# Opening stage of a hybrid decoder step: operands made kind by kind between the products of two blocks, second token half turned through a scaled identity

## The chip, the cores and the metric

One core of one Trainium2 chip. The metric is the device time of one execution in microseconds (us). The kernel before takes 2243.91 us, the median of 3 runs (2242.6 to 2245.94).

## What is computed

One inference step of a decoder trunk with one layer, for 1024 prompt tokens and 32 sample tokens (8 sequences of 4), all float32. In the reference, cut to what the opening touches:

```
h = rmsnorm(x, norm_w)                                       # x: tokens x 1024
pool_in, pool_z, qk_pre, v, o_pre, m_z, if_pre, gate_pre = jnp.split(h @ w_in, SPLIT_OFFSETS, axis=-1)
...
qk, conv_hist_new = causal_conv_silu(qk_pre, conv_hist, conv_w, conv_b)   # 4 taps along the tokens, then silu
q, k = jnp.split(qk, 2, axis=-1)
```

with `rmsnorm(x, w) = x * rsqrt(mean(x * x) + EPS) * w`, the mean over the 1024 features of a token. Behind it stand a pooling branch, a matrix memory (mLSTM) over chunks of 128 tokens, gates, an output projection and a last norm. `w_in` is 1024 features by some 12,000 columns, and the kernel goes through it in blocks of 256 columns.

## The kernel before, in words

**Tokens and halves.** The tokens are cut into two halves of 512 prompt and 16 sample tokens, HH = 528 columns each (`early` and `late`). The 1024 features are 8 tiles of 128 partitions (k = 0 to 7), and h stands with the features on the partitions.

**Products.** A block of w_in (1024 features by 256 columns) is multiplied with all tokens by a scheme of seven products in place of eight: both matrices are cut into 2 x 2 parts, and sums and differences of the parts are multiplied. `OPS` names the h operand of each: product a takes B11 (early tokens, features 0 to 511), 00 takes B21 (early, features 512 to 1023), d takes M1 = B12 - B11 (B12 and B22 are the late tokens' parts), b takes M2 = M1 - B22, c takes T3 = B22 - B12, 10 takes N4 = M2 + B21, 01 takes B22. The weights are combined in `prep`.

**Precision.** Each operand is split into a high part in fp32r and the rest: weights into whi and wlo, h into hh and hl (M2 into m2h and m2l, T3 into t3h and t3l, N4 into n4h and n4l). The high part is made on ScalarE (ACT, `hi`, L363 and L365), the low one on VectorE (DVE, `lo`, L369 and L371). High by high, high by low and low by high are multiplied. With 4 tiles of features and 2 token pieces of 264 (CH) a product is 24 TensorE (PE) matmuls in a FeatBlock (L157: the blocks of q and k, whose output has the columns on the partitions) and 48 in a block of the other form (L215, 256 columns). The first two blocks, 0 and 1, are FeatBlocks of q, ConvBlocks: their results go through the conv (`give`: L315 on ACT, three taps L317 on DVE, the silu L320 and L321 on ACT, then a store).

**The opening.** `norm_in` (L522) loads the four early x tiles of 128 tokens, scales each row by its rstd (L550), turns them on PE (L554, transposes, 4 per k) and splits them into hh and hl; it also keeps a copy of each turned tile, r1 and r2 (L576, L578). `columns` (L480 to L495) loads the small per-feature vectors and conv_w and turns them (L493, L494). `first` runs products a and 00 of block 0. Then the late tiles are loaded into four raw weight buffers, normed and turned, and a loop over k = 0 to 3 makes from each the fourth parts of M1 (L619), B22, T3 (L624), M2 (L627) and N4 (L630), all kinds for one k before the next k.

**Order.** `steps` (L677) is a generator that runs one product at a time, in the order of each block (block 0: a, 00, d, b, c, 01, 10), and prepares weights two or three products ahead. `norm_in` writes down all operands before the products behind 00. The order of instructions on each engine comes from the framework's scheduler, which sees the program as written and places it by its own estimate of times. All loads and stores go through one queue, issued by SyncE (SP), in order. Buffers come from pools with tags: raw weights wraw 7 buffers, whi and wlo 3 each, the work tiles s 6 and z 7, small loads part 2, and in PSUM mm2 3 and misc 2.

After a few products, and at set places, the generator's caller also places the sample rows of the token blocks (`few_part`, L700: 32 matmuls of 32 tokens by 256 columns); the first token block with them is block 2.

## Time and profile before

| | |
|---|---|
| median of 3 runs | 2243.91 us |
| the profiled execution, its own time | 2243.27 us |
| its span (first to last instruction) | 2241.5 us |
| PE busy, matmuls | 96% |
| PEld busy, weight loads | 91% |
| DVE busy | 57% |
| ACT busy | 40% |
| POOL (GpSimd) busy | 5% |
| mean granted clock of PE, as a share | 0.986 |
| instructions | 40008 |

The span is split on each engine into busy and idle time; an idle time ends with an instruction, and the profile names what released that. PE is busy nearly throughout, so its idle time is to be looked for in single stretches. A record's duration is longer than its distance to the next start, since instructions of an engine overlap at their ends; starts are what adds up. The rows that the prediction uses stand in a section of their own below.

### The profile page before, as it was taken

What the parts mean: (1) busy time and instruction counts of PE and PEld (TensorE: products, weight loads), DVE (VectorE), ACT (ScalarE), POOL (GpSimd) and SP (SyncE); (2) the same over time, 40 slices, a digit from 0 to 9 for tenths busy, and PEclk for the clock granted to TensorE, in tenths of its full rate; (3) what the DMA queues carried; (4) which work ended last, traced back from release to release, by engine and by line L of the source; (5) the groups of instructions that cost most, each with busy time, mean ns of one, the idle gap of its engine ahead of it and who ended that gap; (6) DMA issues with size and microseconds to landing.
All of it is one profiled execution on the core that took longest, in us unless ns stands there. A gap on an engine that the chain in (4) does not pass through costs nothing.

```text
span 2241.5 us, 40008 instructions
## 1 busy us (share of the span) xinstructions
PE 2154.4 (96%) x16311; PEld 2045.7 (91%) x16311; DVE 1267.6 (57%) x2184; ACT 903.5 (40%) x1796; POOL 120.2 (5%) x335
## 2 busy tenths in 40 slices
PE   4999999999999999899999899999999999999998
PEld 3899999999999999899999887778778999999998
DVE  7756485556745575536556674575573243543645
ACT  5535454444544453544333342232233331213443
POOL 1100000000100000000000000000000000000000
PEclk8999999999999999999999999999989999999999
DMA  3233323333233321574655645877775343323112
GB/s 129 86 107 120 102 91 110 94 107 116 85 109 110 111 88 41 164 266 143 203 163 177 195 143 168 293 267 252 255 267 171 117 128 110 101 98 111 53 48 83
DMA packets 238600, 312.70 MB, mean 140 GB/s; under 512 B 13994, under 2 KB 170066, under 8 KB 238416
## 3 DMA queue, kind: packets, MB, share of 16 engines
q1 hardware_dynamic: 238416, 310.15, 42.6%
q8 instruction: 128, 2.10, 0.4%
q14 instruction: 56, 0.46, 0.1%
HBM read 200.01 MB, written 110.45 MB: 139 GB/s over the span
## 4 chain that ended last, share of the span: by engine, by line
PE 87%; DMA 6%; DVE 3%; ACT 2%; issue 1%; SPq 1%; POOL 0%; DVEq 0%; POOLq 0%; ACTq 0%
PE mm L215 21%; PE mm L157 15%; PE mm L376 12%; PE mm L378 12%; PE mm L377 12%; PE num L1132 2%; PE misc L917 1%; PE num L376 1%; PE num L377 1%; PE kv L1136 1%; PE num L378 1%; DMA o<-oD 1%; PE kv L376 1%; DMA ct<-state_mlstm_C 1%; PE kv L377 1%; PE kv L378 1%
## 5 line engine op out<-in xcount | busy, mean ns | idle before, releaser
L369 DVE TENSOR_TENSOR wlo<-wraw,whi 128x1024 fp32r<-128x1024 f32 (+1 forms) x220 | 238.4, 1085 | 220.9 <-ACT whi L363 215.5
L363 ACT ACTIVATE whi<-wraw 128x1024 fp32r<-128x1024 f32 (+1 forms) x220 | 209.2, 951 | 348.7 <-PE mm L215 103.4
L376 PE MATMUL mm<-hh,whi 128*128 128x352 f32 (+1 forms) x832 | 264.7, 318 | 12.4 <-ACT sz L1275 6.6
L378 PE MATMUL mm<-hh,wlo 128*128 128x352 f32 (+1 forms) x832 | 262.2, 316 | 0.3 <-DVE wlo L369 0.3
L377 PE MATMUL mm<-hl,whi 128*128 128x352 f32 (+1 forms) x832 | 261.5, 314 | 0.0
L215 PE MATMUL mm<-whi,hl 128*128 128x256 f32 x768 | 216.0, 281 | 0.0
L215 PE MATMUL mm<-wlo,hh 128*128 128x256 f32 x768 | 216.0, 281 | 0.0
L215 PE MATMUL mm<-whi,hh 128*128 128x256 f32 x768 | 214.6, 279 | 0.0
L376 PEld LDWEIGHTS mm<-hh,whi 128*128 128x128 f32 x832 | 158.3, 190 | 25.6 <-ACT sz L1275 8.2
L378 PEld LDWEIGHTS mm<-hh,wlo 128*128 128x128 f32 x832 | 158.2, 190 | 6.8 <-issue 5.0
L377 PEld LDWEIGHTS mm<-hl,whi 128*128 128x128 f32 x832 | 158.7, 191 | 5.7 <-issue 4.4
L157 PE MATMUL mm<-hh,whi 128*128 128x264 f32 x512 | 149.9, 293 | 3.4 <-DVE s L624 2.4
L317 DVE SCALAR_TENSOR_TENSOR z<-z,vcols,z 128x556 f32<-128x556 f32 x192 | 146.7, 793 | 9.5 <-ACT z L315 7.9
L157 PE MATMUL mm<-hl,whi 128*128 128x264 f32 x512 | 147.3, 288 | 0.6 <-DVE hl L371 0.4
L157 PE MATMUL mm<-hh,wlo 128*128 128x264 f32 x512 | 146.7, 286 | 0.0
L215 PEld LDWEIGHTS mm<-whi,hh 128*128 128x128 f32 x768 | 144.7, 188 | 0.0
L215 PEld LDWEIGHTS mm<-whi,hl 128*128 128x128 f32 x768 | 144.6, 188 | 0.0
L215 PEld LDWEIGHTS mm<-wlo,hh 128*128 128x128 f32 x768 | 144.3, 188 | 0.2
L1137 DVE SCALAR_TENSOR_TENSOR ct<-ct,dec,kv 128x512 f32<-128x512 f32 x128 | 93.2, 742 | 73.9 <-PE kv L1136 67.0
L378 PE MATMUL mm<-mvhB,wlo 128*128 128x352 f32 x384 | 123.0, 322 | 0.0
L377 PE MATMUL mm<-mvlB,whi 128*128 128x352 f32 x384 | 122.7, 321 | 0.0
L376 PE MATMUL mm<-mvhB,whi 128*128 128x352 f32 x384 | 121.6, 323 | 0.0
(438 smaller groups left out, 6060.2 us busy)
## 6 DMA issues: line engine op xcount, KB each, us to landing
wraw<-w_in SPq DMA_DIRECT2D x112, 512.0 KB
ct<-state_mlstm_C SPq DMA_DIRECT2D x32, 1024.0 KB
new_C_sample<-ct SPq DMA_DIRECT2D x32, 1024.0 KB
qkD<-z SPq DMA_DIRECT2D x64, 256.0 KB
qk<-qkD SPq DMA_DIRECT2D x16, 1024.0 KB
sgD<-sz SPq DMA_DIRECT2D x16, 528.0 KB
sg<-sgD SPq DMA_DIRECT2D x16, 528.0 KB
vD<-z SPq DMA_DIRECT2D x32, 256.0 KB
```

Of the source, the lines that this page charges most:

```text
L157: self.tr.nc.tensor.matmul(ps[:, j, :CH], lhsT=st[:, k], rhs=mv[k][:, c], start=start and k == 0 and n == 0, stop=stop and k == 3 and n == ...
L215: self.tr.nc.tensor.matmul(ps[:, t // 2, t % 2 * 256:t % 2 * 256 + 256], lhsT=st[k][:, c], rhs=mv[:, k], start=start and t % 2 == 0 and k ...
L317: nc.vector.scalar_tensor_tensor(out=acc, in0=z[:, o:o + tot], scalar=wc(o), in1=acc, op0=ALU.mult, op1=ALU.add)
L363: self.nc.scalar.activation(out, in_, AF.Copy)
L369: self.nc.vector.tensor_tensor(out=out, in0=in_, in1=hi.bitcast(F32), op=ALU.subtract)
L376: mm(ps, lhsT=sh, rhs=mh, start=start, stop=False)
L377: mm(ps, lhsT=sh, rhs=ml, start=False, stop=False)
L378: mm(ps, lhsT=sl, rhs=mh, start=False, stop=stop)
L917: nc.tensor.matmul(out, lhsT=qk[:, 4 + d, i * L:(i + 1) * L], rhs=qk[:, d, i * L:], start=d == 0, stop=d == 3)
L1132: nc.tensor.matmul(num[32 * d:32 * d + 32, 0, :], lhsT=qm[:, b * P + d * NS:b * P + (d + 1) * NS], rhs=ct[:, d, :], start=b == 0, stop=b = ...
L1136: nc.tensor.matmul(kv, lhsT=km[:, d * P:(d + 1) * P], rhs=vst, start=True, stop=True)
L1137: nc.vector.scalar_tensor_tensor(out=ct[:, d, :], in0=ct[:, d, :], scalar=self.dec[:, h * DB + b, 1:2], in1=kv, op0=ALU.mult, op1=ALU.add)
```

## The change

- `take` no longer gives a result to the conv at once while a list `held` is open: the six results that fall into the opening are kept, and their conv (taps and silu) is written down only after T3's operands.
- `prep` makes the weights of d and b together, and those of c and 01, whichever of the two is asked for first.
- `norm_in` loads norm_w first and the early x into the buffers that later hold N4, the late x into those that later hold M2. The copies r1 and r2 go. The late tiles' squares are all on ACT, and their rows are not scaled: a diagonal matrix of the four tiles' rstd (`diag`) is the moving operand of an fp32 matmul that turns and scales at once (`scaled`, L573 to L581); for M1, minus the identity times the early tile is added in the same PSUM group.
- The operands are made kind by kind: all of M1, then three products, B22 and M2, two products, T3 (for which the early tiles are turned again), the held convs, three products, N4 (the early tiles turned again).
- `steps` has a table of the first 14 products, in which blocks 0 and 1 alternate; before, block 1 began when block 0 was done. The caller's count of steps is moved by the 8 steps that `norm_in` now takes itself.

```diff
     def take(self, fh, th, ps, other):
-        self.give(fh, th, self.bring(fh, th, ps, other))
+        x = self.bring(fh, th, ps, other)
+        if self.tr.held is None:
+            self.give(fh, th, x)
+        else:
+            self.tr.held.append((self, fh, th, x))
...
-        elif i == "d":
+        elif i in self.w:
+            return
+        elif i in "db":
...
-        elif i == "c":
+        elif i in ("c", "01"):
...
-        xa = [self.t(xp, [P, 2, D], f"t3{x}") for x in "hl"]
-        junk = self.t(xp, [P, 2, D], "m2h")
-        xs = self.t(xp, [P, 2, D], "m2l")[:, 0, :]
-        tiles = [xa[i // 2][:, i % 2, :] for i in range(4)]
+        x1, x2 = [], []
+        xa = [self.t(xp, [P, 2, D], f"n4{x}") for x in "hl"]
+        xb = [self.t(xp, [P, 2, D], f"m2{x}") for x in "hl"]
+        junk = self.t(xp, [P, 2, D], "t3h")
+        xs = self.t(xp, [P, 2, D], "t3l")
+        v0, xs = xs[:8, 1, :P], xs[:, 0, :]
+        nc.sync.dma_start(v0, I["norm_w"].rearrange("(a b) -> a b", b=P))
         for i in range(4):
-            nc.sync.dma_start(tiles[i], I["x_prompt"][i * P:(i + 1) * P, :])
+            x1.append(xa[i // 2][:, i % 2, :])
+            nc.sync.dma_start(x1[i], I["x_prompt"][i * P:(i + 1) * P, :])
         nc.sync.dma_start(xs[:NS], I["x_sample"])
-        v0 = self.t(g, [P, 512], "part", bufs=2)[:8, :P]
-        nc.sync.dma_start(v0, I["norm_w"].rearrange("(a b) -> a b", b=P))
-
+        def rows_r(i, x, rows):
...
-            if i % 3 == 1:
+            if i % 2 and i < 4:
...
-            r = self.rstd(g, ss[:rows], D, rows)
+            return self.rstd(g, ss[:rows], D, rows)
-        def turned(xs, ps, k):
-            for a, x in enumerate(xs):
-                nc.tensor.transpose(ps[:, a * P:(a + 1) * P], x[:, k * P:(k + 1) * P], self.ident)
+        def turned(ps, k):
+
+            for i, x in enumerate(x1):
+                nc.tensor.transpose(ps[:, i * P:(i + 1) * P], x[:, k * P:(k + 1) * P], self.ident)
+            return ps
+
+        def scaled(ps, k, less):
+
+            f = slice(k * P, (k + 1) * P)
+            for i in range(4):
+                o = ps[:, i * P:(i + 1) * P]
+                nc.tensor.matmul(o, lhsT=x2[i][:, f], rhs=diag[:, i], start=True, stop=not less)
+                if less:
+                    nc.tensor.matmul(o, lhsT=x1[i][:, f], rhs=minus, start=False, stop=True)
             return ps
...
-        r1, r2 = [], []
         for k in range(KT):
             if k % 2 == 0:
                 two = self.mm2()
-            ps = turned(tiles, two[:, k % 2], k)
-            nw = self.nw[:, k:k + 1]
-            both(self.hh[:, k, early], self.hl[:, k, early], ps, nw)
-            r = self.t(xp, [P, HH], f"n4{'hl'[k // 4]}{k % 4}")[:, :HT]
-            if k % 2:
-                nc.scalar.activation(r, ps, AF.Identity, scale=nw)
-            else:
-                nc.vector.tensor_scalar(out=r, in0=ps, scalar1=nw, scalar2=None, op0=ALU.mult)
-            (r1 if k < 4 else r2).append(r)
-
+            both(self.hh[:, k, early], self.hl[:, k, early], turned(two[:, k % 2], k), nw(k))
...
+        part = lambda x, k0, t: [x[:, k, t] for k in range(k0, k0 + 4)]
+        e, l = slice(0, HH), slice(HH, NT)
+        self.ops = dict(B11=(part(self.hh, 0, e), part(self.hl, 0, e)), B21=(part(self.hh, 4, e), part(self.hl, 4, e)),
+                        B22=(part(self.hh, 4, l), part(self.hl, 4, l)), M1=(part(self.hh, 0, l), part(self.hl, 0, l)))
+        def operand(name, tag):
+            x = [self.t(xp, [P, 4, HH], f"{tag}{h}", F32R) for h in "hl"]
+            self.ops[name] = [part(y, 0, slice(0, HH)) for y in x]
+            return x
+
+        def go(n):
+            for _ in range(n):
+                next(blocks)
+        self.held = []
+        go(2)
+        for i in range(4):
+            x2.append(xb[i // 2][:, i % 2, :])
+            nc.sync.dma_start(x2[i], I["x_prompt"][(4 + i) * P:(5 + i) * P, :])
         self.columns()
-        first()
-
-        xb = [self.t(self.wp, [P, D], "wraw", bufs=self.nraw) for i in range(4)]
+
+        zt = lambda: self.t(g, [P, 3 + HH + 28], "z", bufs=self.nz)
+        diag, minus = zt()[:, :512].rearrange("p (i t) -> p i t", i=4), zt()[:, :P]
+        nc.vector.tensor_scalar(out=minus, in0=self.ident, scalar1=-1.0, scalar2=None, op0=ALU.mult)
         for i in range(4):
-            nc.sync.dma_start(xb[i], I["x_prompt"][(4 + i) * P:(5 + i) * P, :])
-        for i in range(4):
...
-        tt = lambda: self.t(g, [P, HH], "s", bufs=self.nsb)[:, :HT]
+            r = rows_r(4 + i, x2[i], P)
+            nc.vector.tensor_scalar(out=diag[:, i], in0=self.ident, scalar1=r, scalar2=None, op0=ALU.mult)
+        vtt, stt = nc.vector.tensor_tensor, nc.vector.scalar_tensor_tensor
+        st = lambda: self.t(g, [P, HH], "s", bufs=self.nsb)[:, :HT]
+
+        ab = self.t(self.wp, [P, 4, 256], "wraw", bufs=self.nraw).rearrange("p (i a) n -> p i (a n)", i=2)
+        a = [ab[:, 0], ab[:, 1], st(), st()]
+        for k in range(4):
+            nc.scalar.activation(a[k], scaled(self.miscps(), k, True), AF.Identity, scale=nw(k))
+            both(self.hh[:, k, late], self.hl[:, k, late], a[k])
+
...
+        both(self.hh[:, 4:, samp], self.hl[:, 4:, samp], s22)
+        go(3)
+
         for k in range(4):
-            nw, nw2 = self.nw[:, k:k + 1], self.nw[:, k + 4:k + 5]
-            two = self.mm2()
-            ps = turned(xb, two[:, 0], k)
-            b12 = tt()
-            nc.scalar.activation(b12, ps, AF.Identity, scale=nw)
-            a = tt()
-            vtt(out=a, in0=b12, in1=r1[k], op=ALU.subtract)
-            both(self.hh[:, k, late], self.hl[:, k, late], a)
-            ps = turned(xb, two[:, 1], k + 4)
-            both(self.hh[:, k + 4, late], self.hl[:, k + 4, late], ps, nw2)
-            b = tt()
-            nc.vector.scalar_tensor_tensor(out=b, in0=ps, scalar=nw2, in1=b12, op0=ALU.mult, op1=ALU.subtract)
-            both(t3[0][:, k, :HT], t3[1][:, k, :HT], b)
-            c = tt()
-            nc.vector.scalar_tensor_tensor(out=c, in0=b, scalar=-1.0, in1=r1[k], op0=ALU.mult, op1=ALU.subtract)
-            both(m2[0][:, k, :HT], m2[1][:, k, :HT], c)
-            e = tt()
-            vtt(out=e, in0=c, in1=r2[k], op=ALU.add)
-            hi, lo = [self.t(xp, [P, HH], f"n4{x}{k}", F32R) for x in "hl"]
-            both(hi[:, :HT], lo[:, :HT], e)
-            both(hi[:, HT:], lo[:, HT:], sums[:, 3, k])
-            n4[0].append(hi)
-            n4[1].append(lo)
-        part = lambda x, k0, s: [x[:, k, s] for k in range(k0, k0 + 4)]
-        early, late = slice(0, HH), slice(HH, NT)
-        self.ops = dict(B11=(part(self.hh, 0, early), part(self.hl, 0, early)),
-                        B21=(part(self.hh, 4, early), part(self.hl, 4, early)),
-                        B22=(part(self.hh, 4, late), part(self.hl, 4, late)),
-                        M1=(part(self.hh, 0, late), part(self.hl, 0, late)),
-                        T3=[[x[:, k] for k in range(4)] for x in t3],
-                        M2=[[x[:, k] for k in range(4)] for x in m2], N4=n4)
+            ps = scaled(self.miscps(), k + 4, False)
+            stt(out=a[k], in0=ps, scalar=nw(k + 4), in1=a[k], op0=ALU.mult, op1=ALU.subtract)
+            both(self.hh[:, k + 4, late], self.hl[:, k + 4, late], ps, nw(k + 4))
...
+        hi, lo = operand("M2", "m2")
+        both(hi[:, :, HT:], lo[:, :, HT:], sums[:, 1])
+        for k in range(4):
+            both(hi[:, k, :HT], lo[:, k, :HT], a[k], -1.0)
+        go(2)
+
+        hi, lo = operand("T3", "t3")
+        both(hi[:, :, HT:], lo[:, :, HT:], sums[:, 2])
+        for k in range(4):
+            x = st()
+            stt(out=x, in0=turned(self.miscps(), k), scalar=nw(k), in1=a[k], op0=ALU.mult, op1=ALU.subtract)
+            both(hi[:, k, :HT], lo[:, k, :HT], x, -1.0)
+        for b, fh, th, z in self.held:
+            b.give(fh, th, z)
+        self.held = None
+        go(3)
+        for k in range(4):
+            stt(out=a[k], in0=turned(self.miscps(), k + 4), scalar=nw(k + 4), in1=a[k], op0=ALU.mult, op1=ALU.subtract)
+        hi, lo = operand("N4", "n4")
+        both(hi[:, :, HT:], lo[:, :, HT:], sums[:, 3])
+        for k in range(4):
+            both(hi[:, k, :HT], lo[:, k, :HT], a[k])
...
-        blocks[0].order = ("a", "00", "d", "b", "c", "01", "10")
-        todo = [(b, n, i) for b in blocks for n, i in enumerate(b.order)]
-        made = 0
-        for n, (b, _, i) in enumerate(todo):
+
+        both = [(0, "a"), (0, "00"), (1, "a"), (1, "00"), (0, "d"), (0, "b"), (0, "01"), (1, "b"), (1, "d"), (0, "c"),
+                (1, "01"), (1, "c"), (0, "10"), (1, "10")]
+        todo = [(blocks[b], i) for b, i in both] + [(b, i) for b in blocks[2:] for i in b.order]
+        made, seen = 0, {}
+        for n, (b, i) in enumerate(todo):
             while made < min(len(todo), n + (2 if n < 2 else 3)):
-                x, k, j = todo[made]
+                x, j = todo[made]
+                k = seen[x] = seen.get(x, -1) + 1
...
-        def first():
-            early = lambda x, k0: [x[:, k, :HH] for k in range(k0, k0 + 4)]
-            self.ops = dict(B11=(early(self.hh, 0), early(self.hl, 0)), B21=(early(self.hh, 4), early(self.hl, 4)))
-            next(blocks)
-            next(blocks)
-        self.norm_in(first)
+        self.norm_in(blocks)
         for n, _ in enumerate(blocks):
-            if n == count - 2 - 4:
+            if n == count - 10 - 4:
```

SP's queue in the opening, before (behind the early x_prompt tiles; x_prompt is the tokens, wraw the raw weight tiles, state_pool to new_pool_sample a copy from input to output, part a small load buffer):

```order
L489 DMA part_267<-conv_b 32x128
L665 DMA wraw_278<-w_in 128x4x256
L665 DMA wraw_280<-w_in 128x4x256
L1169 DMA new_pool_sample<-state_pool 16x704 x3
L491 DMA part_272<-conv_w 128x128
L1169 DMA new_pool_sample<-state_pool 16x704 x4
L593 DMA wraw_373<-x_prompt 128x1024
L593 DMA wraw_374<-x_prompt 128x1024
L593 DMA wraw_375<-x_prompt 128x1024
L593 DMA wraw_376<-x_prompt 128x1024
L1169 DMA new_pool_sample<-state_pool 16x704
L276 DMA part_282<-state_conv 24x256
```

and now:

```order
L282 DMA part_256<-state_conv 24x256
L698 DMA wraw_293<-w_in 128x4x256
L698 DMA wraw_295<-w_in 128x4x256
L282 DMA part_297<-state_conv 24x256
L622 DMA m2h_140<-x_prompt 128x1024 x2
L622 DMA m2l_141<-x_prompt 128x1024 x2
L1205 DMA new_pool_sample<-state_pool 16x704 x8
L496 DMA part_340<-ple_norm_w 8x128
L496 DMA part_340<-pool_scale 8x128
L496 DMA part_340<-mlstm_norm_w 16x128
L496 DMA part_340<-conv_b 32x128
L498 DMA part_345<-conv_w 128x128
```

The second block's weights (wraw_293 and 295) and its history (part_297) now stand ahead of the late x tiles (L622, before L593), behind block 0's own; the pool's copies come behind them, and the vectors and conv_w behind these.

PE at the turns of `columns` up to the first matmul of product a, before (misc_274 takes the vectors and conv_w, mm_78 to mm_87 the turned early tiles, misc_328 the history):

```order
L493 MATMUL misc_274<-ident_112,part_267 128x64
L494 MATMUL misc_274<-ident_112,part_272 128x128
L554 MATMUL mm_78_187<-ident_112,t3h_138 128x128 x2
L554 MATMUL mm_78_187<-ident_112,t3l_139 128x128 x2
L554 MATMUL mm_81_204<-ident_112,t3h_138 128x128 x2
L554 MATMUL mm_81_204<-ident_112,t3l_139 128x128 x2
L554 MATMUL mm_84_221<-ident_112,t3h_138 128x128 x2
L554 MATMUL mm_84_221<-ident_112,t3l_139 128x128 x2
L289 MATMUL misc_328<-ident_112,part_282 128x24 x2
L554 MATMUL mm_87_238<-ident_112,t3h_138 128x128 x2
L554 MATMUL mm_87_238<-ident_112,t3l_139 128x128 x2
L157 MATMUL mm_101_292<-hh_135,whi_284 128x264
```

and now, in product 00 of block 0 (mm_101; mm_82 is the last pair of early tiles, misc_347 takes the vectors and conv_w):

```order
L163 MATMUL mm_101_309<-hh_135,whi_262 128x264
L568 MATMUL mm_82_227<-ident_112,n4h_138 128x128 x2
L568 MATMUL mm_82_227<-ident_112,n4l_139 128x128 x2
L163 MATMUL mm_101_309<-hl_136,whi_262 128x264
L163 MATMUL mm_101_309<-hh_135,wlo_263 128x264
L500 MATMUL misc_347<-ident_112,part_340 128x64
L163 MATMUL mm_101_309<-hh_135,whi_262 128x264
L501 MATMUL misc_347<-ident_112,part_345 128x128
```

The turns of the vectors (L500) and of conv_w (L501) stood ahead of all products and now stand inside product 00.

DVE where the operands are made, before (hl, t3l, m2l and n4l are low parts, s the differences in full precision, mm_142 a turned late tile; one k of the loop):

```order
L371 SCALAR_TENSOR_TENSOR hl_136<-mm_142_459,vcols_122,hh_135 128x512
L624 SCALAR_TENSOR_TENSOR s_476<-mm_142_459,vcols_122,s_464 128x512
L369 TENSOR_TENSOR hl_136<-s_466,hh_135 128x512
L627 SCALAR_TENSOR_TENSOR s_480<-s_476,n4h_80_202 128x512
L369 TENSOR_TENSOR t3l_410<-s_476,t3h_409 128x512
L630 TENSOR_TENSOR s_484<-s_480,n4l_86_236 128x512
L369 TENSOR_TENSOR m2l_412<-s_480,m2h_411 128x512
L369 TENSOR_TENSOR n4l_149_487<-s_415,n4h_148_486 128x16
L619 TENSOR_TENSOR s_499<-s_497,n4h_82_211 128x512
L369 TENSOR_TENSOR n4l_149_487<-s_484,n4h_148_486 128x512
```

and now, at the end of M2 and in T3 (misc_654, 663 and 672 are early tiles turned again, wraw_382 and s_383 hold M2 negated in full precision, z_695 and z_709 are conv sums of held results):

```order
L665 SCALAR_TENSOR_TENSOR s_653<-misc_654,vcols_122,wraw_382 128x512
L376 TENSOR_TENSOR wlo_759<-wraw_293,whi_758 128x1024
L179 TENSOR_TENSOR z_647<-mm_142_516,s_621 128x528
L378 SCALAR_TENSOR_TENSOR t3l_650<-s_653,t3h_649 128x512
L323 SCALAR_TENSOR_TENSOR z_695<-z_334,vcols_122,z_695 128x556
L665 SCALAR_TENSOR_TENSOR s_662<-misc_663,vcols_122,wraw_382 128x512
L323 SCALAR_TENSOR_TENSOR z_709<-z_508,vcols_122,z_709 128x556
L665 SCALAR_TENSOR_TENSOR s_671<-misc_672,vcols_122,s_383 128x512
```

All kinds of one k followed one another; now T3's parts come after all of M2, and the taps of the held results (L323, before L317) lie between them, with the low weights of a later product (wlo_759) ahead.

## Rows read from the trace of the kernel before

**Rows 1.** The page, part 1: busy time of each engine, share of the span.

```profile
PE 2154.4 (96%) x16311; PEld 2045.7 (91%) x16311; DVE 1267.6 (57%) x2184; ACT 903.5 (40%) x1796; POOL 120.2 (5%) x335
```

**Rows 2.** Stretches of 20 us: PE, PEld, DVE, ACT, POOL busy, PEclk, DMA, GB/s.

```profile
40.00:60.00 20.00, 8.54 (x33) 5.97 (x32) 19.13 (x33) 12.39 (x25) 1.45 (x3) 0.57 0.03 13
60.00:80.00 20.00, 18.28 (x132) 17.26 (x131) 13.79 (x22) 9.89 (x21) 1.60 (x5) 0.91 0.34 106
```

**Rows 3.** The chain of waits: start us, duration us, what.

```profile
18.42 6.72 DMA part<-state_conv
...
66.88 0.61 DVE m2l L369
...
67.54 13.62 PE mm L157 x110
...
110.87 1.86 PE misc L700 x32
```

**Rows 4.** The timeline of PE in product a of block 0: start us, duration us.

```profile
30.13 0.42 PE L157 MATMUL mm<-hl,whi 128*128 128x264 f32 x1
30.35 0.42 PE L157 MATMUL mm<-hh,wlo 128*128 128x264 f32 x1
...
33.87 0.28 PE L157 MATMUL mm<-hl,whi 128*128 128x264 f32 x1
33.99 0.28 PE L157 MATMUL mm<-hh,wlo 128*128 128x264 f32 x1
```

**Rows 5.** The timeline of DVE: start us, duration us.

```profile
23.84 1.21 DVE L369 TENSOR_TENSOR wlo<-wraw,whi 128x1024 fp32r<-128x1024 f32 x1
24.98 1.39 DVE L371 SCALAR_TENSOR_TENSOR hl<-mm,vcols,hh 128x512 fp32r<-128x512 f32 x2
...
33.47 0.22 DVE L607 TENSOR_TENSOR s<-hs 128x64 f32<-128x64 f32 x1
...
43.90 0.74 DVE L624 SCALAR_TENSOR_TENSOR s<-mm,vcols,s 128x512 f32<-128x512 f32 x1
44.56 0.79 DVE L317 SCALAR_TENSOR_TENSOR z<-z,vcols,z 128x556 f32<-128x556 f32 x1
45.26 0.68 DVE L369 TENSOR_TENSOR hl<-s,hh 128x512 fp32r<-128x512 f32 x1
45.87 0.68 DVE L627 SCALAR_TENSOR_TENSOR s<-s,n4h 128x512 f32<-128x512 f32 x1
```

**Rows 6.** The timeline of ACT: start us, duration us, idle before and releaser.

```profile
4.07 1.06 ACT L548 ACTIVATE m2h<-t3h 128x1024 f32<-128x1024 f32 x1 [1.99 <-DMA t3h<-x_prompt]
...
33.45 1.06 ACT L363 ACTIVATE whi<-wraw 128x1024 fp32r<-128x1024 f32 x1 [3.93 <-PE mm L157]
34.41 0.59 ACT L164 ACTIVATE s<-mm 128x528 f32<-128x528 f32 x1
...
49.84 0.61 ACT L363 ACTIVATE n4h<-s 128x512 fp32r<-128x512 f32 x1
50.37 0.67 ACT L365 ACTIVATE hh<-mm,vcols 128x512 fp32r<-128x512 f32 x1
```

**Rows 7.** The timeline of PE at L917, and the forms of that line.

```profile
975.42 2.78 PE L917 MATMUL misc<-qk 128*128 128x256 f32 x16
977.95 0.41 PE L376 MATMUL mm<-hh,whi 128*128 128x352 f32 x1
...
L917 PE MATMUL misc<-qk x256: 272/326/454, 975.4 to 1325.0; 128*128 128x256 f32 x64, 128*128 128x128 f32 x64
```

**Rows 8.** The timeline of SP's queue: two issues in one row.

```profile
0.80 0.87 SPq L537 DMA_DIRECT2D t3h<-x_prompt  x2
```

**Rows 9.** Waits of SP's queue up to 140 us: total us, times, longest us.

```profile
SPq L276 <- DMA vSD<-part: 2.4, 1, 2.4
```

**Rows 10.** Busy time by stretches of 4 us, columns as in rows 2.

```profile
20.00:24.00 4.00, 2.23 (x8) 1.43 (x8) 4.00 (x9) 2.52 (x6) 0.00 (x0) 1.00 0.74 286
...
64.00:68.00 4.00, 2.43 (x18) 2.02 (x17) 3.96 (x8) 2.45 (x5) 0.00 (x0) 1.00 1.08 364
```

26 lines of the change are left out of this document (11 added, 15 removed).

## The prediction

> **What bounds the kernel now.** I read the page first. TensorE (PE) is busy for 96% of the span, VectorE (DVE) 57% [rows 1]: the program is PE-bound, and only stretches in which PE waits can give time back. The table of busy time by 20 us stretches shows where that is: from 40 to 60 us PE's records fill 8.54 us at a granted clock of 0.57, while DVE is busy for 19.13 of 20 us; in the next stretch PE comes back to 18.28 [rows 2]. So the opening is bound by DVE, which makes the operands. The chain of waits gives the border: its last step on DVE is the low half of M2's fourth tile at 66.88 us; from 67.54 on it is PE alone up to the 32 small matmuls of the sample rows of the first token block (L700) at 110.87 us [rows 3]. The order of instructions after that point is the same before and after, except for a few neighbours, so I compare one moment: when PE reaches those 32.
>
> Up to 67.54 PE has done 82 of the 336 products (L157) of the first two blocks: a, 00 and d of block 0 with 24 each, and 10 of b. In the 43.3 us to 110.87 it does the other 254 and 96 token products (L215) without a wait. A product costs 0.122 us at the full clock (33.87 to 33.99 us) and 0.22 just after PE has come out of idle time (30.13 to 30.35), 2.4 and 1.2 GHz [rows 4].
>
> **The change, step by step.**
>
> *Removed and moved.* DVE loses four row scalings and two squarings of the late x tiles, four copies of the early tiles and the separate a, c and e sums; ACT gets the squarings. At DVE's prices, taken from one start to the next (0.66 us for 512 columns out of PSUM, 0.61 out of SBUF, 1.14 for 1024 columns [rows 5]), that is some 10 us, but it counts only where DVE ends last. Both blocks' conv taps (0.70 us each [rows 5]) now come only after T3 has begun, and block 1's a and 00 fill PE while the late half is made. PE gets 48 more fp32 matmuls of 128 columns. I walk the chain as the new order has it.
>
> *A. Loads.* The queue now holds block 1's weights before the late x, and pool copies and the vectors behind. The last late tile is 6.47 MB into the queue. It moved 286 GB/s in one full stretch and 364 in another [rows 10]; I take 325, between them. The first tile of 0.52 MB was there at 4.07 us [rows 6], 2.5 more than its bytes need, and one issue of 0.44 us (0.87 for two [rows 8]) is now ahead of it: 2.9 + 19.9 = 22.8 us (25.5 at 286). Behind it one pool copy and four vector loads are issued, 2.2 us. For a small load no row is exact: a small store was waited for 2.4 us [rows 9], and the history load that stood behind the late x took 6.72 us [rows 3]. I take 2.4, since the queue is empty by then, and keep 6.72 for the bound. The vectors land at 27.4. The conv_w load is put into the same buffer that L500's transpose has to read first, so it is issued after that: 27.4 + 0.44 + 2.4 = 30.2. Its transpose stands in the middle of block 0's 00 product, and PE stops there. Without this stop the product could go on at 28.4, when the eighth early tile is split. Product a itself can start at about 21 us, several us sooner than now, which gains nothing, as PE runs into the stop anyway. A ends at 30.5.
>
> *B. PE.* 14 products of block 0's 00, 24 of block 1's a, 6 of its 00: 44 x 0.122 = 5.4. Then the first scaled group, 8 fp32 matmuls. The nearest rows are the 16 plain fp32 matmuls of L917 (8 of 256, 8 of 128 columns): 2.53 us to the next start, 0.105 per 128 columns [rows 7]. 8 x 0.105 = 0.8. B ends at 36.7.
>
> *C. ACT* reads the group out of PSUM and splits it, 0.67 + 0.61 [rows 6]: 38.0. The remaining 40 scaled matmuls, 4.2 us, lie beside D.
>
> *D. DVE,* 30 instructions back to back up to M2's fourth low half: 11 of 512 columns out of SBUF (6.7), 3 of 1024 (3.4), 9 out of PSUM (5.9), 7 slivers of sample columns (0.22 long alone [rows 5], closer in a row: 1.0). 17.0, to 55.0 us. PE has 54 products (6.6) and 40 scaled matmuls there and waits for DVE in between.
>
> *E. A round trip.* Behind that half PE still runs 14 products, 4 transposes and 14 more (3.8, the first of them from 54.4): block 0's b ends at 58.2. ACT can make the next high weights only then, because there are three such buffers, and saves b: 0.96 + 0.59 [rows 6], 59.8. DVE makes the low weights (to 60.3) and adds one result (0.66): 61.0. DVE idles for some 4 us here.
>
> *F. DVE* again, 20 instructions to T3's fourth low half: 9 taps (6.3), 5 out of SBUF (3.1), 5 out of PSUM (3.3), one of 1024 (1.1): 13.8, to 74.8 us.
>
> *G. PE.* Left are 28 products of the two c and 72 of 01, 10, 10: 100 instead of 254, with the same 96 of L215. 43.3 - 154 x 0.122 = 24.5: 99.3. From 64 to 75 us PE has only some 19 products and 20 transposes; in rows 2 the clock stood at 0.57 over a thin stretch, so I add one more climb, 19 products at 0.22: 1.9. PE reaches L700 at **101.2**.
>
> 110.87 - 101.2 = 9.7 us. The sum is made against the profiled execution, 2243.27 us with a span of 2241.5; the median of the three runs is 0.64 above it. 2243.27 - 9.7 = **2233.6 us**. A measurement of this kernel tells some 0.2%, 4.5 us, from no change.
>
> **The rivals.**
>
> *1. PE waits long for conv_w, and the result is slower.* Each us that it lands later shifts B to G by one. Against it: a small transfer of 2.4 us [rows 9]. For it: the 6.72 us of a small load in a full queue [rows 3], twice instead of 2.4 (+8.6), and the late x at 286 GB/s (+2.7): conv_w ready at 41.8, 2244.9 us. Even is at 40.2, clearly slower past 44.7.
>
> *2. The multiplying fp32 matmul is dearer than turning.* If it took four times 0.105, B would grow by 2.5 us, and PE in D would need 6.6 + 40 x 0.42 = 23.4 us instead of the 18.3 that C and D last: +5.1. Gain 2.1: 2241.2. Against it: the plain multiplying matmuls of L917 run at 0.105 [rows 7]. The Trainium skill (TensorE: Matmul & The Clock Gate, Terms) says that on trn2 a weight load and matmul have a transpose mode that is four times faster for FP32; by it the time would be this rival's, but the rows of L917 show no such factor for multiplying.
>
> *3. PE stays at the low clock from 40 to 75 us,* as it did for most of 40 to 60 [rows 2]. D's 10.8 us of PE work would become 21.6 against 18.3, and E's 3.8 would double: +3.3 + 3.8. Gain 2.6: 2240.7. For it: PE waits again and again in D and F; against it: it has more than twice the work of the old stretch.
>
> *4. More is gained.* The clock is kept up (1.9) and conv_w is there before 28.4 (2.1): gain 13.7, 2229.6. For it: 364 GB/s [rows 10] brings the late x at 20.7.
>
> **How the numbers follow.** Forecast 0.60 (its own range 2230 to 2238), rival 4 0.18, rival 3 0.12, rival 1 0.07, rival 2 0.03. The range reaches from below rival 4 to rivals 2 and 3: 2228 to 2241.5, and leaves out rival 1 and a tail below. Faster by over 0.2%: the forecast, rival 4 and a quarter of rival 3, 0.81. Slower by over 0.2%: the far part of rival 1, 0.05. Within: 0.14.
>
> **What would show it.** In the profile after: the first product near 21 us; PE waiting for the conv_w load inside block 0's 00 product until about 30; hardly an idle gap on DVE from 38 to 55, one of about 4 us before 60 that ends on ACT's high weights, none from 61 to 75; the last long wait of PE ending near 75 on T3's low half; L700 near 101 instead of 110.87; scaled matmuls at 0.105 us each. The sum is wrong if PE idles in the opening for another reason, if conv_w comes after 34 us, or if a difference shows behind L700.

## The result and the profile after

The changed kernel took **2232.36 us** in the median of 4 runs (2231.08 to 2234.49), the kernel before, in the same comparison, 2244.77 us (4 runs, 2242.60 to 2245.94): a ratio of 0.9947 [0.9933, 0.9962]. The forecast was 2233.6 us. The profiled execution took 2232.33 us with a span of 2230.6; before, 2243.27 and 2241.5. One slip stands ahead of the prediction: three results of the opening are held back from the conv, not six (nine taps of L323, at three taps each, run between 63.70 and 75.60 us).

Part 1 of the page of the changed kernel, which answers to [rows 1]:

```profile
PE 2159.6 (97%) x16407; PEld 2054.8 (92%) x16407; DVE 1257.2 (56%) x2172; ACT 900.8 (40%) x1791; POOL 122.7 (6%) x335
```

Its busy time by stretches of 20 us (columns as in [rows 2], which it answers):

```profile
20.00:40.00 20.00, 18.24 (x146) 17.38 (x146) 12.17 (x24) 9.84 (x18) 2.73 (x8) 1.00 0.12 37
40.00:60.00 20.00, 18.93 (x149) 17.69 (x149) 15.05 (x28) 10.75 (x23) 0.32 (x2) 1.00 0.29 79
60.00:80.00 20.00, 15.79 (x109) 14.45 (x108) 18.66 (x28) 14.08 (x27) 1.79 (x3) 0.91 0.20 66
```

PE has 96 records more than before. From 40 to 60 us it is busy for 18.93 us at the full clock, where it had 8.54 at 0.57, and DVE has fallen from 19.13 to 15.05. The gap is not gone: the thin stretch now lies from 60 to 80 us.

The chain of waits (start us, duration us, what):

```profile
21.01 4.05 PE mm L163 x31
...
26.11 1.75 DMA part<-conv_w
27.90 0.33 PE misc L501
28.23 5.36 PE mm L163 x44
...
41.03 0.95 ACT whi L370
42.01 1.00 DVE wlo L376
...
58.61 1.61 PE mm L163 x13
60.24 1.07 ACT whi L370
61.34 1.22 DVE wlo L376
...
76.39 0.61 DVE t3l L378
77.05 3.68 PE mm L163 x28
...
101.22 1.86 PE misc L736 x32
```

The last step on DVE is T3's low half at 76.39 us (M2's at 66.88 before), and the 32 sample matmuls start at 101.22 instead of 110.87 [rows 3]: **9.65 us of the 10.9** that the two profiled executions differ by lie ahead of this moment. I call it T* below. Behind it the executions took 2132.4 us (before) and 2131.1.

A second moment splits the 9.65 us. In both kernels PE has to stop inside the second product (00 of block 0) and then goes on with the first `hl,whi` matmul of its rest; I call that the *resumption*. Here is what PE and the others did from the resumption to T*: before,

```profile
36.88:110.87 73.99, 60.43 (x440) 56.24 (x444) 60.16 (x87) 43.76 (x89) 7.96 (x23) 0.86 0.24 73
```

and in the changed kernel:

```profile
27.99:101.22 73.23, 67.95 (x537) 65.18 (x541) 60.94 (x95) 42.68 (x86) 12.36 (x23) 0.98 0.21 66
```

The resumption came 8.89 us earlier, and the way from it to T* got only 0.76 us shorter. On that way PE's waiting fell from 13.56 us to 5.28 and its clock rose from 0.86 to 0.98, but its busy time went up by 7.52 us. So the new order did what it should for the waits, and something on PE took nearly all of it back: 97 matmul records more on this way (537 and 440), at 0.111 us each 10.8 us, less what the higher clock gave back.

### The profile page after: what moved, and what is told of

Its sections match the earlier page's. It is cut to its first block, busy times and chain, and to the rows that moved or that the text cites. A ratio compares the mean times of both kernels' runs of the same rounds, so it can differ in the third digit from the quotient of the medians.

```text
span 2230.6 us, 40176 instructions
## 1 busy us (share of the span) xinstructions
PE 2159.6 (97%) x16407; PEld 2054.8 (92%) x16407; DVE 1257.2 (56%) x2172; ACT 900.8 (40%) x1791; POOL 122.7 (6%) x335
## 4 chain that ended last, share of the span: by engine, by line
PE 87%; DMA 6%; DVE 3%; ACT 2%; SPq 1%; issue 1%; POOL 0%; DVEq 0%; POOLq 0%; ACTq 0%
PE mm L221 21%; PE mm L163 14%; PE mm L383 12%; PE mm L385 12%; PE mm L384 12%; PE num L1168 2%; PE misc L953 2%; PE num L383 1%; PE kv L383 1%; PE num L384 1%; PE num L385 1%; PE kv L384 1%; PE kv L385 1%; PE kv L1172 1%; DMA o<-oD 1%; DMA ct<-state_mlstm_C 1%
## 5 line engine op out<-in xcount | busy, mean ns | idle before, releaser
L323 DVE SCALAR_TENSOR_TENSOR z<-z,vcols,z 128x556 f32<-128x556 f32 x192 | 146.8, 794 | 8.4 <-ACT z L321 6.6
```

Source lines behind the costliest of these rows:

```text
L323: nc.vector.scalar_tensor_tensor(out=acc, in0=z[:, o:o + tot], scalar=wc(o), in1=acc, op0=ALU.mult, op1=ALU.add)
```

## The experiments

| kernel | resumption | T* | between | median us (runs) | ratio to before |
|---|---|---|---|---|---|
| before | 36.88 | 110.87 | 73.99 | 2244.77 (4) | 1 |
| changed | 27.99 | 101.22 | 73.23 | 2232.36 (4) | 0.9947 [0.9933, 0.9962] |
| again | 29.49 | 102.68 | 73.19 | 2233.67 (6) | 0.9955 [0.994, 0.9971] |
| again2 | 27.93 | 101.15 | 73.22 | 2233.12 (6) | 0.9948 [0.9934, 0.9961] |
| cols_first | 27.35 | 100.57 | 73.22 | 2231.07 (6) | 0.9953 [0.9937, 0.997] |
| own | 29.52 | 102.76 | 73.24 | 2233.89 (7) | 0.9959 [0.9943, 0.9974] |
| t3_first | 28.42 | 100.68 | 72.26 | 2232.90 (7) | 0.9963 [0.9947, 0.9978] |
| at_once | 27.61 | 101.20 | 73.59 | 2231.96 (4) | 0.995 [0.9935, 0.9965] |
| block_order | 34.24 | 107.60 | 73.36 | 2241.46 (10) | 0.9992 [0.998, 1.0003] |
| row_diff | 27.84 | 94.79 | 66.95 | 2233.98 (8) | 0.9962 [0.9949, 0.9976] |
| row_again | 29.67 | 96.61 | 66.94 | 2231.08 (5) | 0.9951 [0.9937, 0.9964] |
| row_cols | 31.93 | 97.27 | 65.34 | 2228.47 (5) | 0.9936 [0.9923, 0.9948] |
| row_own | 29.55 | 95.67 | 66.12 | 2230.13 (6) | 0.9938 [0.9925, 0.9951] |
| before_own | 36.45 | 110.47 | 74.02 | 2242.81 (12) | 0.9992 [0.9981, 1.0003] |

Resumption and T* are of the profiled execution, one per kernel. The runs come from five comparisons, in which the median of the kernel before lay between 2242.2 and 2244.8 us; across them the ratios compare, not the medians. Diffs are against the changed kernel, but for `before_own`.

### again, again2: the changed kernel once more

> The changed kernel once more, unaltered, as the control for the others. PE reached the 32 sample matmuls (L736) at 101.22 us in its first profile, 9.65 us sooner than before (110.87), while its whole time was 10.9 us shorter. Theory: the whole gain lies in the opening and that moment is a property of the program; expected again 101.2 within 0.5 us, ratio to before about 0.995. Rival: loads and clock scatter; then the moment moves by 2 us or more and no difference below that can be read from one trace.

> The changed kernel a third time, as the control on the same chip. Its sample matmuls stood at 101.22 and 102.68 us in two profiles, and the 1.46 between them was there already when conv_w landed (27.9 and 29.4). Theory: the moment is the landing of conv_w plus 73.3 us, whatever that is here. Rival: other waits scatter too, and the distance differs by over 0.5 us.

T* came at 102.68 and 101.15 us. The 1.5 us of `again` were there at the resumption already; from there to T* the three executions of this kernel agree within 0.04 us. The cause shows in PE's timeline of product a (start us, duration us). `again`:

```profile
21.66 0.42 PE L163 MATMUL mm<-hh,whi 128*128 128x264 f32 x1
21.88 0.42 PE L163 MATMUL mm<-hl,whi 128*128 128x264 f32 x1
```

and the first execution of the changed kernel:

```profile
21.36 0.29 PE L163 MATMUL mm<-hh,wlo 128*128 128x264 f32 x1
21.48 0.29 PE L163 MATMUL mm<-hh,whi 128*128 128x264 f32 x1
```

Some 17 products of `again` stand 0.22 us apart instead of 0.12. L500 comes behind product a on PE, the conv_w load is issued only after L500, and the rest of 00 waits for that load: L500 ran 1.43 us later than in the first execution (27.27 and 25.84), and T* came 1.46 later.

### row_diff: scale and subtract in rows, then only turn

```diff
-                nc.tensor.matmul(o, lhsT=x2[i][:, f], rhs=diag[:, i], start=True, stop=not less)
-                if less:
-                    nc.tensor.matmul(o, lhsT=x1[i][:, f], rhs=minus, start=False, stop=True)
+                nc.tensor.transpose(ps[:, i * P:(i + 1) * P], x2[i][:, k * P:(k + 1) * P], self.ident)
...
-            nc.vector.tensor_scalar(out=diag[:, i], in0=self.ident, scalar1=r, scalar2=None, op0=ALU.mult)
+            nc.vector.scalar_tensor_tensor(out=u, in0=u, scalar=r, in1=x1[i][:, :512], op0=ALU.mult, op1=ALU.subtract)
+            nc.vector.tensor_scalar(out=v, in0=v, scalar1=r, scalar2=None, op0=ALU.mult)
```

`u` and `v` are the two halves of a late tile's 1024 columns, `diag` and `minus` go.

> The scaled identity is taken out: the late tiles are scaled by rows on DVE again, the first 512 features as late x r - early in one instruction (4 of 512 columns out of SBUF, 0.61 each), the others scaled (4 more, at most 0.61 each), and turned by 32 transposes. PE loses 96 records of 0.111 (10.7 us) and gets 32 of 0.11 (3.5 us); DVE gets up to 4.9 us in place of five slivers of 0.13. Theory: DVE was idle for most of 24 to 36 us and takes the scalings there, and the scaled groups made DVE wait (41.2 to 42.0, 49.8 to 50.3, 51.1 to 51.7 us) and started it 1.3 us later; the sample matmuls come 2 to 3 us sooner, at 98 to 99.5. Rival (what the change seems to be for): the scaled identity relieves DVE, which bounds the opening; without it they come 3 to 5 us later, at 104 to 106.

First the price itself. PE's timeline of the changed kernel at the first scaled group:

```profile
33.44 0.38 PE L576 MATMUL misc<-z,m2h 128*128 128x128 f32 x2
33.66 0.39 PE L578 MATMUL misc<-z,n4h 128*128 128x128 f32 x2
33.88 0.39 PE L576 MATMUL misc<-z,m2h 128*128 128x128 f32 x2
...
36.92 0.37 PE L163 MATMUL mm<-hh,whi 128*128 128x264 f32 x1
```

and the line's own view (duration min/median/max in ns, first and last start):

```profile
L576 PE MATMUL misc<-z,m2h x32: 270/275/377, 33.4 to 50.9; 128*128 128x128 f32 x32
L576 PE MATMUL misc<-z,m2l x32: 275/275/275, 34.3 to 51.4; 128*128 128x128 f32 x32
```

L576 is written 32 times and leaves 64 records, L578 16 times and leaves 32; each pair goes from 33.44 to 33.66, 0.22 us. One fp32 matmul that multiplies leaves two records of 0.11 us. In `row_diff` the same line only turns:

```profile
L574 PE MATMUL misc<-ident,m2h x16: 270/272/418, 25.4 to 44.5; 128*128 128x128 f32 x16
L574 PE MATMUL misc<-ident,m2l x16: 270/272/418, 26.0 to 44.7; 128*128 128x128 f32 x16
```

32 transposes, 32 records. From the resumption to T*:

```profile
27.84:94.79 66.95, 61.38 (x469) 58.97 (x472) 59.46 (x90) 42.74 (x86) 13.56 (x22) 0.95 0.24 72
```

PE's busy time is 6.57 us shorter than in the changed kernel, its waiting 0.29 longer, the way 6.28 shorter. 64 records fewer at 0.111 are 7.1 us, and four of the transposes have moved ahead of the resumption (the record count falls by 68); the lower clock, 0.95, takes some of it back. T* comes at 94.79. The other 32 of the 96 records are the early tiles turned again for T3 and N4, 3.5 us; no run took those out. Against the kernel before, which also turns by plain transposes, the way is 7.0 us shorter: about that much is what the new order of the opening as a whole is worth behind the resumption. DVE does the scaling and subtracting from 20 to 40 us, where it now is busy for 18.73 us instead of 12.17; there it had room. `row_again` is the same kernel again, for its total time:

> The row difference with plain transposes once more, unaltered. Its first profile had the sample matmuls 7.9 us sooner than the control, their last group still 7.8 us sooner at 850 us, but the end only 3.4 us sooner, and its median was level with the control's. View 1: the loss behind 850 us was scatter of the transfers in those two profiles; in this one the end comes 5 to 9 us sooner than the control's 2231.9. View 2: it is of the program; the end again comes at 2228 to 2231, with the loss between 1180 and 1650 us.

66.94 us between the two moments, T* at 96.61, since its resumption came at 29.67. But of the 6.4 and 4.6 us that T* came earlier the totals show little: `row_diff` took 2233.98 us where `again`, in the same comparison, took 2233.67, and `row_again` 2231.08, at a ratio of 0.9951 to the kernel before. More on that below.

### own and cols_first: without the stop for conv_w

`own` loads the vectors and conv_w into an unused part of the sample tokens' buffer, so that conv_w needn't wait for L500:

```diff
-        v1 = self.t(self.gp, [P, 512], "part", bufs=2)[:64, :P]
+        v1 = self.spare[:64, 1, 2 * P:3 * P]
...
-        v2 = self.t(self.gp, [P, 512], "part", bufs=2)[:, :P]
+        v2 = self.spare[:, 1, P:2 * P]
```

`spare` is that buffer. `cols_first` issues these loads ahead of the late x instead:

```diff
+        self.columns()
         self.held = []
...
-        self.columns()
```

> The changed kernel with a place of its own for the vectors and for conv_w (in the unused half of the sample tokens' buffer), so that conv_w is issued with the vectors, and all five ahead of the pool's copies, without pushing the late x back. Theory (step A: the stop in product 00 is on the chain): PE goes on as soon as the eighth early tile is split, at 27.0 instead of 28.2 to 29.7, and the sample matmuls come at 100.0 (27.0 plus 73.0), 1.2 to 2.7 us sooner than the controls. Rival: another wait takes its place, and they stay at 101 to 102.7.

> The vectors and conv_w are loaded and turned ahead of block 0's product a, as before the change, instead of inside product 00. In the changed kernel's trace PE resumed product 00 at 28.2 us, after conv_w, and the eighth early tile's low half was there at 27.0. Theory (the chain of steps A to G of the prediction holds): PE resumes about 1.2 us sooner and so does each later step, the sample matmuls at 100.0 instead of 101.2. Rival: the stop is covered, because later steps end on ACT and DVE; the moment stays within 0.4 us of the control. Second rival: the six loads push the late x and block 1's weights back by 2 to 3 us and the moment comes later than the control.

PE's timeline of `own` (in brackets the idle time ahead, and who ended it):

```profile
28.73 0.39 PE L163 MATMUL mm<-hh,whi 128*128 128x264 f32 x1 [0.54 <-ACT hh L372]
29.52 0.39 PE L163 MATMUL mm<-hl,whi 128*128 128x264 f32 x1 [0.40 <-DVE hl L378]
```

and of `cols_first`:

```profile
27.35 0.39 PE L163 MATMUL mm<-hl,whi 128*128 128x264 f32 x1 [0.40 <-DVE hl L378]
```

The stop at conv_w is gone in both, and the split of the eighth early tile is what PE now waits for. In `cols_first` that is at 27.35 us, 0.64 ahead of the changed kernel, and T* moves by 0.65. In `own` product a was one of the slow kind (20 products 0.22 us apart), the eighth tile was turned that much later, and nothing was won. So the stop is worth 0.6 us: right behind it stands another.

### before_own: the kernel before, without its late history load

The kernel before with vectors, conv_w and norm_w loaded into m2l's unused half, so that the history load of [rows 3] isn't behind them:

```diff
-        v1 = self.t(self.gp, [P, 512], "part", bufs=2)[:64, :P]
+        v1 = self.spare[:64, 1, 2 * P:3 * P]
...
-        v2 = self.t(self.gp, [P, 512], "part", bufs=2)[:, :P]
+        v2 = self.spare[:, 1, P:2 * P]
...
-        v0 = self.t(g, [P, 512], "part", bufs=2)[:8, :P]
+        v0 = self.spare[:8, 1, :P]
```

> The kernel before, with one thing of the change's opening alone: the vectors, conv_w and norm_w are loaded into the unused half of the sample tokens' buffer, so that the history load no longer waits for their buffer behind the late x, and PE does not stop for it from 18.42 to 25.15 us ahead of product a. Operands, products and their order stay. In the kernel before, product 00 resumed at 36.88 us and the sample matmuls came 73.99 later; in three profiles of the changed kernel they came 73.2 after the same point, which stood at 27.9 to 29.5. View S (the gain is the earlier start): product 00 resumes some 5 us sooner, near 32, and the sample matmuls come 74 later, at 104 to 106: half of the change's gain or more by the place of two loads. View O (the operands, which DVE made one k after another until 67.5 us, set the end, as the prediction has it): an earlier start is worth no more than the 3 us that DVE stood idle from 33 to 40 us, and the moment comes at 107.9 or later.

The resumption moved from 36.88 to 36.45, T* from 110.87 to 110.47, the time by nothing that can be told. So it wasn't the late load that held the resumption in the kernel before. PE's timeline of `before_own` shows what PE waits for instead, ahead of product a:

```profile
22.48 0.69 PE L555 MATMUL mm<-ident,t3h 128*128 128x128 f32 x2 [0.91 <-DVE n4l L579]
25.99 0.69 PE L555 MATMUL mm<-ident,t3h 128*128 128x128 f32 x2 [2.39 <-ACT n4h L577]
27.67 0.59 PE L157 MATMUL mm<-hh,whi 128*128 128x264 f32 x1 [0.56 <-ACT n4h L577]
```

L577 and L579 (L576 and L578 in the kernel before) make the copies r1 and r2 of the turned early tiles. From 17 us to product a five of PE's waits end on them here, 4.2 us together; in the kernel before three, 4.0 us, beside 2.54 for the history load. By the code the copy is the last reader of a turned tile in PSUM, and the next turns and product a need one of the three buffers (mm2) of these tiles. The changed kernel has no such copies, and its product a starts at 21.01 us instead of 28.44 (27.67 in `before_own`): 7.43 of the 8.89 us. The other 1.46 us are the pace behind it. In the kernel before some 18 products of a stand 0.22 us apart [rows 4], and it is 8.44 us from the start of a to the resumption; in the first execution of the changed kernel it is 6.98, in `again`, where some 17 are slow, 8.66.

The other candidate is DVE's queue: squarings and scalings of late tiles stood in it ahead of the last split of an early tile, and from 8 to 28 us DVE was busy for 16.63 us before and for 13.74 after. `row_diff` speaks against it. It scales the late tiles on DVE again, all eight instructions ahead of that split (L378):

```profile
25.98 0.75 DVE L624 SCALAR_TENSOR_TENSOR m2l<-m2l,rs_r,n4l 128x512 f32<-128x512 f32 x1
26.64 0.48 DVE L625 TENSOR_SCALAR m2l<-m2l,rs_r 128x512 f32<-128x512 f32 x1
27.04 0.74 DVE L378 SCALAR_TENSOR_TENSOR hl<-mm,vcols,hh 128x512 fp32r<-128x512 f32 x1
```

The busy time from 8 to 28 us (columns as in [rows 2]), in the kernel before and in `row_diff`:

```profile
8.00:28.00 20.00, 9.26 (x39) 6.09 (x40) 16.63 (x34) 12.91 (x25) 3.95 (x6) 1.00 0.66 214
8.00:28.00 20.00, 16.02 (x83) 12.19 (x84) 17.90 (x39) 14.61 (x30) 5.37 (x9) 1.00 0.71 240
```

DVE is busier there than in the kernel before, and the resumption still comes at 27.84 us. So the copies are the cause that is left for most of the earlier start. That is read from the waits, not shown: a run that takes the copies alone away was not made.

### t3_first, at_once: what holding the conv is worth

`t3_first` also makes the conv taps and block 1's weights of 01 and c wait for T3's last low half, by adding zero times T3 to three columns of their inputs (the taps' here, the weights' likewise):

```diff
-            nc.gpsimd.tensor_copy(z[:, 0:3], self.last[f])
+            if tr.held:
+                nc.vector.scalar_tensor_tensor(out=z[:, 0:3], in0=tr.t3, scalar=0.0, in1=self.last[f], op0=ALU.mult,
+                                               op1=ALU.add)
+            else:
+                nc.gpsimd.tensor_copy(z[:, 0:3], self.last[f])
```

`at_once` holds nothing and has the loads of `cols_first`:

```diff
-        self.held = []
+        self.columns()
+        self.held = None
...
-        for b, fh, th, z in self.held:
-            b.give(fh, th, z)
-        self.held = None
```

> The order on DVE alone is altered: the conv taps of the held results and the low half of block 1's weights for 01 and c are made to come after T3's fourth low half, by giving each a small instruction that reads T3 (the sums are the same, four slivers more). In the changed kernel DVE stood idle from 56.9 to 61.3 us for those weights and then ran nine taps of 0.70 between T3's parts, whose last low half came at 76.9; PE idled or ran at the low clock for some 8 us between 62 and 77. Theory: T3 set the end; its last half now comes at 63 to 66 us, PE's idle time goes, and the sample matmuls come 3 to 6 us sooner, at 95 to 98. Rival: the work is only moved, N4 and the weights behind it wait for the same taps, and PE waits there instead: the moment stays at 101 within 1 us.

> The results of the opening are given to the conv at once, as before the change, instead of being held until T3 is written (with the vectors and conv_w loaded ahead, which the conv needs then, so its control is cols_first: sample matmuls at 100.6 us). Three results are concerned, nine taps of 0.70. Theory: in the changed kernel these nine taps stand before T3's last low half all the same, and the stretch up to M2 was bound by PE's scaled matmuls with some 4 us of DVE time to spare there; so holding them gains nothing, and the moment stays at 100.6 within 1 us or comes up to 2 us sooner. Rival (what the list is for): six taps, 4.2 us, now stand ahead of M2 on a DVE that sets the end, and the moment comes 4 us later, at 104 to 106.

In `t3_first` T3's last low half was made at 68.13 us instead of 76.31, 8.2 us earlier, and T* came 0.5 earlier (the way from the resumption is 1.0 shorter). The waits came back behind it, as PE's timeline shows (L166 is the products' line here, L182 adds a result, L386 splits):

```profile
73.30 0.36 PE L166 MATMUL mm<-n4h,whi 128*128 128x264 f32 x1 [1.43 <-DVE z L182]
74.34 0.39 PE L166 MATMUL mm<-hh,wlo 128*128 128x264 f32 x1 [0.68 <-DVE wlo L386]
84.85 0.36 PE L224 MATMUL mm<-whi,hh 128*128 128x256 f32 x1 [0.58 <-DVE z L182]
86.06 0.29 PE L344 MATMUL misc<-ident,new 128*27 128x128 f32 x1 [0.85 <-POOL new L328]
```

`at_once` has its resumption at 27.61 and T* at 101.20: 73.59 us, 0.37 more than its control `cols_first` (73.22). Whether the taps come before or after T3, DVE owes them before T*.

### block_order: without the alternation

```diff
-        both = [(0, "a"), (0, "00"), (1, "a"), (1, "00"), (0, "d"), (0, "b"), (0, "01"), (1, "b"), (1, "d"), (0, "c"),
-                (1, "01"), (1, "c"), (0, "10"), (1, "10")]
+        both = [(0, "a"), (0, "00"), (0, "d"), (0, "b"), (0, "01"), (0, "c"), (0, "10"), (1, "a"), (1, "d"), (1, "b"),
+                (1, "00"), (1, "c"), (1, "01"), (1, "10")]
```

The two places that take three products each take one, and the caller's count is moved by 4.

> The products of blocks 0 and 1 no longer alternate: block 0 does a, 00, d, b, 01, c, 10 between the operands (kind by kind as in the change), then block 1 follows. Theory: the filling of PE is what the table brings. DVE and ACT have block 1's weights less to make before T3 (six instructions of 512 or 1024 columns, one block result and three taps, some 9 us), so T3's last low half comes up to 9 us sooner, near 68; but PE has done only 5 of the 14 products by then instead of about 10, and 116 matmuls more (14.2 us) lie behind it: sample matmuls at 104 to 108. Rival: DVE alone sets the end, and with less to do for T3 the moment comes at 95 to 101.

T* came at 107.60, about where this was expected, but for another reason. PE's timeline:

```profile
23.61 0.48 PE L501 MATMUL misc<-ident,part 128*128 128x128 f32 x1 [2.98 <-DMA part<-conv_w]
...
34.24 0.39 PE L163 MATMUL mm<-hl,whi 128*128 128x264 f32 x1 [0.46 <-DVE hl L378]
```

With this table the scheduler put conv_w's transpose ahead of early tiles, so the resumption was 6.25 us late; from there to T* it is 73.36 us, as with the alternation. The run doesn't show the alternation to be worth anything, and, as the order ahead of the resumption moved with it, not that it is worth nothing.

### row_cols, row_own: the better versions

`row_diff` with the loads of `cols_first`, and with those of `own`.

> The row difference with plain transposes in place of the scaled identity, and the vectors and conv_w ahead of the first product, together. Theory: the opening is a chain, and both add up: sample matmuls at 93 to 94.5 us (94.8 and 0.7 to 1 less). For the whole time two views: (1) what the opening saves reaches the end, then the time is 7 us below the control of the changed kernel, 2225 to 2227; (2) the stages behind 1180 us, whose waits are on loads of o, v and the state (1.7 to 3 us of PE's idle time each, longest transfers 7 to 9 us), take most of it back, then it is 2230 to 2234 although the moment is 7 us sooner.

> The row difference with plain transposes, and the place of their own for the vectors and conv_w. In the first profile with the row difference PE stopped 1.12 us for conv_w and ran at half clock from 28 to 32 us behind that, and the sample matmuls stood at 94.8; with the loads put first instead, late x came later and they stood at 97.3. Theory: both savings add when no load is pushed back, 92 to 94 us. The order of the late stages is the one of the changed kernel here but for a few neighbours, so the saving should reach the end: 2224 to 2227 us, some 8 below the control. Rival: the late stages, whose waits are on transfers, take back more than 4 us of it: 2228 to 2232.

2228.47 us (0.9936) and 2230.13 us (0.9938) are the lowest medians and ratios of all; the changed kernel, in the same comparison as `row_own`, took 2233.12 (`again2`), 3.0 more. The intervals overlap, so this lead is likely rather than certain. In `row_cols` 16 of the 32 transposes of late tiles stand ahead of the resumption, in `row_own` 8, so these resumptions are later points of the work, and T* is the number to compare.

**What stays open.** T* moved by 4 to 6.4 us in the four `row_` kernels, the medians by 3.9 at most, and in `row_diff` not at all. Profiled time less T* is 2131.1 us in the changed kernel, 2131.2 in `row_cols`, but 2134.2 in `row_own`, 2135.4 in `row_diff` and 2134.5 in `row_again`. The scheduler's order of the late stages differs in `row_diff` from the changed kernel's, hardly in `row_own`. The order alone doesn't take the 3 to 4 us: `cols_first` has the order of `row_diff` there, instruction for instruction on DVE, ACT and SP (compared from 10 us behind T*), and the smallest rest of all kernels, 2129.6 us. And one execution can't tell 3 to 4 us in this rest: in `own`, whose late order is nearly the changed kernel's, it is 2139.2 (its profiled execution, 2241.98 us, is its slowest). Whether the `row_` kernels lose anything behind T* stays open.

## Why the prediction was right, and where it was not

The time was right (1.2 us below the forecast), T* to 0.02 us, and that by luck: A and G were 2.5 and 2.1 us too long, B with C, D and E 1.3, 2.4 and 0.9 too short, and these cancel. The next execution of the same kernel had T* at 102.68. By the steps:

- **A (30.5) failed by its size:** 27.99. The vectors were there when L500 ran at 25.84, not at 27.4, and conv_w took 1.75 us instead of 2.4 plus issue. That the product stops there for conv_w was right; that it was the stop that counts was not: without it PE waits at 27.35 for the eighth tile (`cols_first`).
- **A's sentence that the earlier product a "gains nothing" fell.** conv_w is issued behind L500, L500 runs behind product a, and so does the eighth tile's turn; a later a made a later T* (`again`, `own`). The earlier start of product a is 7.43 us of the gain. What held it back before, the copies' hold on PSUM, had no term in my sum: I counted the copies only as DVE's time. My own sum had 6.4 us of the gain in the earlier resumption and 3.3 in a shorter way from it (101.2 - 30.5 = 70.7); the runs have 8.9 and 0.8.
- **B failed by its price:** 0.105 us for a scaled matmul, measured 0.223. The rows of L917 [rows 7] were misread: the 16 records there are 8 matmuls, two records each. 48 matmuls cost PE 10.7 us, where 32 transposes cost 3.5 (4 in 0.44). ACT began at 35.42 (C), 7.4 us behind A instead of 6.2.
- **D (17.0 us) failed by its overlap.** It called DVE bound with PE beside it. Even at 0.223 us the 54 products and 40 scaled matmuls are only 15.5 us of PE, less than D's 17.0; yet M2's fourth low half came after 19.4 us, at 56.2. DVE waited 2.0 us in four places, 0.9 for ACT's high weights and 1.1 for scaled groups:

```profile
50.30 0.75 DVE L650 SCALAR_TENSOR_TENSOR s<-misc,vcols,s 128x512 f32<-128x512 f32 x1 [0.46 <-PE misc L576]
51.68 0.75 DVE L650 SCALAR_TENSOR_TENSOR s<-misc,vcols,s 128x512 f32<-128x512 f32 x1 [0.63 <-PE misc L576]
```

- **E held in its mechanism:** DVE's gap of 4.39 us ends on ACT's high weights (chain, 61.34). It took 6.9 us instead of 6.0: PE was 0.8 later with b, counted from M2, and the low weights were 1024 columns wide, 1.1 us instead of 0.5; ACT's part was 0.45 shorter.
- **F held:** 13.8 us, from 63.1 to 76.9, as summed.
- **G held but for its last term.** From 76.9 us to T* it is 24.3, and the sum without the climb of the clock was 24.5. The climb was there, but not behind T3: the granted clock was 0.60 from 72 to 76 us (row at the end), while DVE was still at T3's parts, so the 1.9 us that I added for it were not paid.
- **Rivals.** 1: conv_w landed at 27.86, not at 41.8. 2 was half true: the multiplying matmul costs twice 0.105, not four times. The Trainium skill (TensorE: Matmul & The Clock Gate, Terms) speaks of a transpose mode four times faster for FP32. Here turning costs 0.111 us and multiplying 0.223 for the same 128 columns, a factor of two. 3: the clock was 1.00 from 20 to 60 us. 4: conv_w was there before 28.4 and the clock's 1.9 us were not paid, as it has it, but B to E took the gain back.

In one sentence: the forecast's cause, fewer waits in the opening, is there (13.56 to 5.28 us), but the scaled identity took most of it back on PE (6.3 us by `row_diff`), and the gain that is measured lies in the earlier resumption, most of it in the earlier start of product a, for which the traces leave the missing copies r1 and r2 as the cause.

## What to carry to other kernels

Take the price of a matmul from the matmuls that the code writes, not from the profile's records: count both. Compare two orders from the last event that they have in common to the next one; the totals hide gains and losses that cancel. Moving work from a vector engine to PE pays only where PE waits; here, where the waits were closed, the 6.6 us put on PE came back as 6.3 us of the way to T*, and moving held work (`t3_first`, `at_once`) mostly moved the wait. Ask of every extra copy what buffer it holds, and who waits for that buffer.

## What the runs showed that was not expected

- An fp32 matmul with a multiplying operand is two records of 0.111 us, a transpose of the same tile one.
- The first products after the early transposes stood 0.22 us apart for none, some 17 and none of the matmuls in three executions of the changed kernel, and for some 20 in `own`, while the stretch's granted clock reads 1.00 (11 records in 2 us, in the row of `again` below). In `again` this shifted T* by 1.5 us.
- After a thin stretch (1.26 us of PE in the 4 us up to 72) the granted clock was 0.60 in the next 4 us, with products at 0.22 us up to 74.55; it lay beside DVE's work on T3.

The busy time of `again` from 22 to 24 us (columns as in [rows 2]):

```profile
22.00:24.00 2.00, 2.00 (x11) 2.00 (x10) 1.20 (x3) 2.00 (x4) 0.45 (x1) 1.00 0.20 51
```

and of the changed kernel from 68 to 76 us:

```profile
68.00:72.00 4.00, 1.26 (x6) 0.84 (x7) 4.00 (x7) 2.10 (x4) 0.49 (x1) 0.97 0.00 0
72.00:76.00 4.00, 4.00 (x21) 3.87 (x22) 4.00 (x6) 1.37 (x3) 0.00 (x0) 0.60 0.28 110
```
